# Strassen products in the second up product and in both down products, quad-shaped down weights, and the squares of x after the first product

## The chip, the cores and the metric

The kernel runs on one core of a Trainium2 chip. The core has a matrix engine (PE), a vector engine (DVE), a scalar engine (ACT), a general engine (POOL) and a queue engine (SP) that issues the transfers; each works through its own instructions in a fixed order and waits for the others by semaphores. The metric is the device time of one execution in microseconds; smaller is better. Before the change it is 2578.58 us, the median of three runs (2578.54 to 2579.13).

## What is computed

The reference is two transformer-like blocks in float32, one after the other, on 256 rows of 2048 columns. The change touches the feed-forward parts of both and the first norm. Cut to these:

```python
# first block
h = rmsnorm(x, norm_mix_g)
proj = h @ w_in
...                                  # two kinds of attention, cross attention
hf = rmsnorm(x, norm_ffn_g)
x = x + (silu(hf @ w_gate) * (hf @ w_up)) @ w_down       # 2048 -> 5632 -> 2048
x = rmsnorm(x, norm_f_g)
# second block
...                                  # gating unit, linear recurrence, w_out
h = rmsnorm(x, norm2_g)
up = causal_dwconv(h @ ffn_w_up, ffn_conv_w, ffn_conv_b)  # 2048 -> 2 x 6144
gate, val = split(up)
x = x + (gelu(gate) * val) @ ffn_w_down                   # 6144 -> 2048
x = rmsnorm(x, final_g)
```

## The kernel before

**Every product in three matmuls.** A float32 operand is split in a high part, rounded to the matrix engine's fast format, and a low part, the rest. `mm3` (L195 to L197) adds high times high, high times low and low times high. So each product of a 128 x 128 block of activations with a 128 x 512 block of weights is three matmuls of 128 x 512.

**Weights.** Each transfer (`fetch`, L279) brings a tile `w` of 128 x 2048, 1 MB. `push` cuts it in pieces of 128 x 1024 and splits each: ACT casts the high part `wh` (L177), DVE subtracts to get the low part `wl` (L178). `half` keeps the piece in use and four more ahead of it; `wh` and `wl` have five buffers each, so a cast waits until the matmuls of the piece five places back are done. The list `seq` sets the order of all tiles.

**A quad.** In the two up products (`w_gu`: gate and up of the first block, `w_uv`: of the second) one tile `w` holds two blocks of 128 rows by two blocks of 512 columns (one of the gate, one of the up half). With two blocks of tokens and two blocks of rows this is a 2 x 2 by 2 x 2 block product. Of kind "N" it takes 8 block products, 24 matmuls, and two weight pieces (0 and 1). Of kind "S" it takes 7, by Strassen's scheme, 21 matmuls, and four weight pieces: "a" (128 x 1024, raw), "c" (128 x 512, raw, its split in plain `r` tiles) and "b" and "d" (128 x 1024, sums in the tiles `wt`, made by DVE at L307, L311 and L312). An S quad also needs sums of activations, which the class `Quad` makes (L119 to L126). Strings of eight letters say which of a group's eight quads is which: `KINDS` "NSNSNSNN" for `w_gu`, 11 groups; `KINDS2` "NNNSNNNN" for `w_uv`, 12 groups.

**Up groups.** `quad_group` runs `gemm_q` over eight quads into four accumulators of the pool `psg` (tiles `pg`) and three of the pool `pss` (tiles `pp`); each pool has four banks. When the last S quad is through, `early` reads three of them (L460 to L462); at the group's end `finish` reads the others in five DVE operations (L468 to L474).

**Down products.** `w_down` and `w_down2` are taken in parts of the hidden width, `PARTS` and `PARTS2`, three each, the down product of a part after its up groups. Before the change they are plain: `gemm_tm` (four groups of 512 columns, two `pg` accumulators each, so that two groups fit in the four banks), and `add_x` (L511) adds the two results to x. No Strassen there. The activations for a part are transposed and split by `ffn_pairs` (first block) or, after the convolution, by `conv_pairs` (second block, lines L1122, L1125, L1137, L1143); these run as generators, one step at each `tick`, beside the next group's matmuls.

**The start.** `x_gen` loads x transposed in eight tiles of 128 x 512; `load_split` splits each for the first product (L180 on ACT, L181 on DVE), squares it on ACT (L552) and has POOL add the square to a sum (L554). The sum gives the first norm's factors.

**What sets the order.** The program is written for all engines at once; a scheduler that simulates time while building decides in which order each engine's instructions stand. On the chip that order is fixed.

## Time and profile before

| what | value |
|---|---|
| median of the runs | 2578.58 us |
| the profiled execution itself | 2578.38 us |
| its span, first to last instruction | 2576.7 us |
| PE, instructions | 12209 |
| DVE, instructions | 2257 |
| granted clock of PE over the span | 0.999 |
| time of the first up product (`w_gu`), one group | 42.4 us |
| time of the second up product (`w_uv`), one group | 44.8 us |
| bytes read from memory | 486.39 MB |

The profile is of one execution. A page gives busy times and shares; the windows view gives the same for chosen stretches, in us from the start of the span; the lines view groups instructions by source line and gives the mean duration of one, and after the second bar the time in which the engine was idle before them, with what it waited for; the timeline gives single instructions with their start and duration. An instruction's duration is not the time until the next one may start: both PE and DVE start the next one earlier, so rates are read from the distances of starts.

### The profile page before, as it was taken

How to read it: one execution, taken by the hardware profiler on the slowest of the kernel's cores; microseconds unless marked ns; L12 is line 12 of the kernel's file. 1: busy time of each engine (PE TensorE's matmuls, PEld its weight loads, DVE VectorE, ACT ScalarE, POOL GpSimd, SP SyncE). 2: the span in 40 equal slices, each digit the busy share in tenths (PEclk: the TensorE clock that was granted, in tenths of full speed). 3: DMA queues.
4: the chain of work that ended last, by engine and by line, in shares of the span. 5: the costliest groups of instructions: out<-in, count | busy, mean ns of one | idle time of the engine just before them, and what ended most of it. 6: DMA issues, size and time to landing. Idle time of an engine off the chain costs nothing.

```text
span 2576.7 us, 31159 instructions
## 1 busy us (share of the span) xinstructions
PE 2557.1 (99%) x12209; PEld 2144.2 (83%) x12209; DVE 1813.8 (70%) x2257; ACT 1397.2 (54%) x1863; POOL 39.5 (2%) x41
## 2 busy tenths in 40 slices
PE   8999999999999999999999999999999999999998
PEld 7888888888888888888888888888888888888887
DVE  7666566556569875887588667866887578757874
ACT  6555554455456553555455555665565456535654
POOL 2000010000000000000000000000000000000000
PEclk9999999999999999999999999999999999999999
DMA  6455555554454555555555564555555554555553
GB/s 258 164 180 204 203 206 182 194 180 164 147 180 180 213 197 195 196 201 197 192 194 213 196 221 163 186 190 184 192 187 190 190 191 178 195 193 194 182 212 131
DMA packets 72723, 490.51 MB, mean 190 GB/s; under 512 B 8192, under 2 KB 8320, under 8 KB 14592
## 3 DMA queue, kind: packets, MB, share of 16 engines
q1 hardware_dynamic: 72576, 488.52, 53.1%
q8 instruction: 96, 1.57, 0.2%
q14 instruction: 51, 0.42, 0.0%
HBM read 486.39 MB, written 2.10 MB: 190 GB/s over the span
## 4 chain that ended last, share of the span: by engine, by line
PE 98%; issue 0%; DVE 0%; ACT 0%; DMA 0%; POOL 0%; SPq 0%; ACTq 0%; POOLq 0%; DVEq 0%
PE pg L195 25%; PE pg L197 25%; PE pg L196 25%; PE pg L364 10%; PE pg L368 5%; PE pp L197 2%; PE pp L196 2%; PE pp L195 2%; PE pp L188 1%; PE pp L1137 1%; DMA w<-in_w_in_f_dram 0%; DVE r L181 0%; DVE wl L178 0%; PE pp L958 0%; PE pp L1010 0%
## 5 line engine op out<-in xcount | busy, mean ns | idle before, releaser
L178 DVE TENSOR_TENSOR wl<-w,wh 128x1024 fp32r<-128x1024 f32 x854 | 1044.5, 1225 | 601.2 <-ACT wh L177 596.1
L177 ACT CAST wh<-w 128x1024 fp32r<-128x1024 f32 x854 | 897.6, 1052 | 872.7 <-PE pg L197 696.0
L196 PE MATMUL pg<-wl,r 128*128 128x512 f32 x2783 | 1085.1, 390 | 0.0
L197 PE MATMUL pg<-wh,r 128*128 128x512 f32 x2783 | 1081.0, 390 | 0.0
L195 PE MATMUL pg<-wh,r 128*128 128x512 f32 x2783 | 1075.5, 391 | 0.0
L197 PEld LDWEIGHTS pg<-wh,r 128*128 128x128 f32 x2783 | 522.4, 188 | 108.2
L196 PEld LDWEIGHTS pg<-wl,r 128*128 128x128 f32 x2783 | 522.6, 188 | 107.3
L195 PEld LDWEIGHTS pg<-wh,r 128*128 128x128 f32 x2783 | 522.6, 188 | 106.6
L364 PE MATMUL pg<-r,wh 128*128 128x512 f32 x1152 | 311.9, 397 | 10.9 <-ACT wh L177 7.2
L364 PEld LDWEIGHTS pg<-r,wh 128*128 128x128 f32 x1152 | 201.7, 190 | 43.5 <-ACT wh L177 7.2
L368 PEld LDWEIGHTS pg<-r,wl 128*128 128x128 f32 x1152 | 168.7, 190 | 17.9
L368 PE MATMUL pg<-r,wl 128*128 128x256 f32 x1152 | 176.8, 284 | 0.0
L178 DVE TENSOR_TENSOR wl<-wt,wh 128x1024 fp32r<-128x1024 f32 x90 | 109.7, 1219 | 39.6 <-ACT wh L177 39.0
L177 ACT CAST wh<-wt 128x1024 fp32r<-128x1024 f32 x90 | 94.7, 1052 | 68.0 <-PE pg L197 40.5
L1125 DVE SCALAR_TENSOR_TENSOR f<-pp,pr,f 128x255 f32<-128x255 f32 x192 | 90.4, 478 | 13.7 <-ACT f L1122 11.7
L1122 ACT ACTIVATE f<-pp,pr 128x256 f32<-128x256 f32 x96 | 53.3, 561 | 33.0 <-PE pp L1137 16.9
L177 ACT CAST r<-f 128x512 fp32r<-128x512 f32 (+1 forms) x88 | 51.5, 585 | 14.9 <-DVE f L484 8.7
L178 DVE TENSOR_TENSOR r<-f,r 128x512 fp32r<-128x512 f32 (+1 forms) x88 | 56.6, 643 | 3.5 <-ACT r L177 2.8
L195 PE MATMUL pp<-wh,r 128*128 128x512 f32 x147 | 58.3, 400 | 0.0
L197 PE MATMUL pp<-wh,r 128*128 128x512 f32 x147 | 57.3, 390 | 0.0
L196 PE MATMUL pp<-wl,r 128*128 128x512 f32 x147 | 57.3, 390 | 0.0
L307 DVE TENSOR_TENSOR wt<-w 128x1024 f32<-128x1024 f32 x45 | 54.8, 1218 | 2.6 <-DMA w<-in_w_gu_dram 2.6
(193 smaller groups left out, 1465.1 us busy)
## 6 DMA issues: line engine op xcount, KB each, us to landing
w<-in_w_uv_dram SPq DMA_DIRECT2D x96, 1024.0 KB, 4.8
w<-in_w_down_dram SPq DMA_DIRECT2D x92, 1024.0 KB, 4.8
w<-in_w_gu_dram SPq DMA_DIRECT2D x88, 1024.0 KB, 4.8
w<-in_w_in_t_dram SPq DMA_DIRECT2D x40, 1024.0 KB, 4.8
w<-in_w_in_f_dram SPq DMA_DIRECT2D x39, 1024.0 KB, 4.8
w<-in_w_o_dram SPq DMA_DIRECT2D x16, 1024.0 KB, 4.8
w<-in_w_xk_dram SPq DMA_DIRECT2D x16, 1024.0 KB, 4.8
w<-in_w_xv_dram SPq DMA_DIRECT2D x16, 1024.0 KB, 4.8
```

Of the source, the lines that this page charges most:

```text
L177: A.copy(hi, src)
L178: V.tensor_tensor(lo, src, hi.bitcast(F32), ALU.subtract)
L188: T.transpose(pt[:, k, t * P:(t + 1) * P], src[t][:, c + k * P:c + (k + 1) * P], ident)
L195: T.matmul(out, lhsT=lh[0], rhs=rh[0], start=start, stop=False)
L196: T.matmul(out, lhsT=lh[0], rhs=rh[1], start=False, stop=False)
L197: T.matmul(out, lhsT=lh[1], rhs=rh[0], start=False, stop=stop)
L307: V.tensor_tensor(sums["b"], b[:, 3:4, :].to_broadcast([P, 2, 512]), b[:, 0:3:2, :], ALU.subtract)
L364: T.matmul(ps[m], lhsT=hi[k][:, m * P:(m + 1) * P], rhs=ops[k].both(k % 2), start=begin and k == 0, stop=stop, skip_group_check=True)
L368: T.matmul(ps[m][:, S:], lhsT=lo[k][:, m * P:(m + 1) * P], rhs=ops[k].hi(k % 2), start=False, stop=False, skip_group_check=True)
L1122: A.activation(y[:, j, :], z[:, j, :], AF.Identity, scale=col("ffn_conv_w_2", 192 + c), bias=col("ffn_conv_b_2", c))
L1125: V.scalar_tensor_tensor(y[:, j, d:], z[:, j, :S - d], col("ffn_conv_w_2", 96 * (2 - d) + c), y[:, j, d:], ALU.mult, ALU.add)
L1137: T.transpose(pt[:, k, t * P:(t + 1) * P], z[t][:, (2 * p + k) * P:(2 * p + k + 1) * P], ident)
```

## The change

- `KINDS2` has two S quads per group of `w_uv` instead of one (places 2 and 5 instead of 3).
- Both down weights are stored as quads too, of two blocks of 128 rows by two blocks of 512 neighbouring columns. `gemm_sum` takes two groups of 1024 columns instead of four of 512. In the first two parts, places 3 and 5 of each eight quads are S (`KINDS_DOWN`); in the last part all are N. The last 1024 columns of the last part of `w_down2` stay plain, as `w_down2_t`.
- `add_quads` takes the place of `add_x`: it uses four `pg` accumulators and, with S quads, four `pp` ones. When the last S quad is through, `early` copies one, makes four combinations and adds them to x; at the end four more additions go to x. From the first to the last S quad of a down group no generator steps.
- Activations that meet an S quad of a down product are made as a `Quad` (the old kind "N" of that class is now called "D").
- The convolution's generator steps faster for the last up group of a part (`pause` 1 instead of 2).
- The squares of x come after the first product's matmuls in the program, and DVE adds them instead of POOL.

```diff
-KINDS2 = "NNNSNNNN"
+KINDS2 = "NNSNNSNN"
+KINDS_DOWN = "NNNSNSNN"
...
-        seq += [(w_down, g, u) for g in range(4) for u in range(g0, g1)]
+        seq += [(w_down, g, u) for g in range(2) for u in range(2 * g0, 2 * g1)]
...
-        seq += [(w_down2, g, u) for g in range(4) for u in range(g0, g1)]
+        seq += [(w_down2, g, u) for g in range(2) for u in range(2 * g0, 2 * g1)] if g0 < PARTS2[-1][0] else []
+    g0, g1 = PARTS2[-1]
+    seq += [(w_down2, 0, u) for u in range(2 * g0, 2 * g1)]
+    seq += [(w_down2_t, g, u) for g in range(2) for u in range(g1 - g0)]
...
     def kind(w, u):
+        if w is w_down or w is w_down2:
+            return KINDS_DOWN[u % 8] if u < 2 * (PARTS if w is w_down else PARTS2)[-1][0] else "N"
...
+    def gemm_sum(wap, g, acts, k0, sums_done):
+        M = {}
+        n = len(acts)
+        ks = [kind(wap, k0 + u) for u in range(n)]
+        first, end = ks.index("S") if "S" in ks else n, n - ks[::-1].index("S") if "S" in ks else 0
...
+        def prod(m, a, b):
+            if m not in M:
+                M[m] = gps() if m > 10 else sps()
+            done[m] += 1
+            mm3(M[m], a, b, done[m] == 1, done[m] == total[m])
+
+        for u in range(n):
+            if u == first:
+                for v in range(first, end):
+                    need(acts, v)
+            a = need(acts, u)
+            if ks[u] == "N":
+                plan = [(0, [(11, a.blk(0, 0), 0), (11, a.blk(1, 0), 1), (21, a.blk(0, 1), 0), (21, a.blk(1, 1), 1)]),
+                        (1, [(22, a.blk(1, 1), 0), (22, a.blk(0, 1), 1), (12, a.blk(1, 0), 0), (12, a.blk(0, 0), 1)])]
+            else:
+                plan = [("a", [(1, a.blk(0, 0), 0), (11, a.blk(1, 0), 1)]),
+                        ("c", [(12, a.sums(3), 0)]),
+                        ("b", [(5, a.sums(0), 0), (7, a.sums(2), 1)]),
+                        ("d", [(6, a.sums(1), 0), (21, a.blk(1, 1), 1)])]
+            for i, ops in plan:
+                hi, lo = half(wap, g, k0 + u, i, 512)
+                for m, x, b in ops:
+                    prod(m, x, (hi[b], lo[b]))
+                if not first <= u < end:
+                    tick()
+            if u == end - 1:
+                sums_done(M)
+        return M
...
+    def add_quads(wap, g, acts, k0):
+        def early(M):
+            m, u2, u3, v = (flat(ft()) for _ in range(4))
+            A.copy(m, M[1])
+            V.tensor_tensor(u2, M[6], m, ALU.add)
+            V.tensor_tensor(u3, M[7], u2, ALU.add)
+            V.tensor_tensor(u2, M[5], u2, ALU.add)
+            V.tensor_tensor(v, M[5], u3, ALU.add)
+            for x, f in zip(parts, (m, u3, v, u2)):
+                V.tensor_tensor(x, x, f, ALU.add)
+
+        parts = [xs(0, 2 * g), xs(1, 2 * g), xs(1, 2 * g + 1), xs(0, 2 * g + 1)]
+        M = gemm_sum(wap, g, acts, k0, early)
+        for x, i in zip(parts, (11, 21, 22, 12)):
+            V.tensor_tensor(x, x, M[i], ALU.add)
...
     def load_split(f, gname, p, sq):
         a = Pair(True).fill(f, [col(gname, 2 * p + j) for j in range(2)])
+        if sq is not None:
+            square(f, sq)
+        return a
+
+    def square(f, sq):
         s = ft()
         A.activation(s, f, AF.Square)
-        if sq:
-            G.tensor_tensor(sq[0], sq[0], s, ALU.add)
-        else:
-            sq.append(s)
-        return a
+        sq.append(s)
+
+    def sum_squares(sq, eng):
+        while len(sq) > 1:
+            eng.tensor_tensor(sq[0], sq[0], sq.pop(1), ALU.add)
...
     ps_q = gemm_fm(w_in_f, 0, h_a)
     al = big(alibi)
+    for f in fs:
+        square(f, sq1)
+        sum_squares(sq1, V)
...
-        for g in range(4):
-            add_x(gemm_tm(w_down, g, acts, g0), g)
-            if g1 == PARTS[-1][1]:
-                spawn(next_in(g, h2_a, sq_f, gg, second_norm), 1)
+        for g in range(2):
+            add_quads(w_down, g, acts, 2 * g0)
+            if last_part:
+                for i in range(2):
+                    spawn(next_in(2 * g + i, h2_a, sq_f, gg, second_norm), 1 + 2 * i)
...
+            if sums and KINDS_DOWN[i + p] == "S":
+                acts[i + p] = Quad("S", y[0], psum=False)
+            else:
+                acts[i + p] = Pair(False).fill(y[0])
...
-            for g in range(4):
-                add_x(gemm_tm(w_down2, g, acts, g0), g)
+            for g in range(2):
+                add_quads(w_down2, g, acts, 2 * g0)
...
+    add_quads(w_down2, 0, acts, 2 * PARTS2[-1][0])
     for g in range(3):
-        add_x(gemm_tm(w_down2, g, acts, PARTS2[-1][0]), g)
+        if g == 2:
+            add_x(gemm_tm(w_down2_t, 0, acts), 2)
```

How the scheduler places this, at three places. In the rows, names with a number are buffers: `wl` and `wh` the low and high parts of a weight piece, `wt` the summed weights, `r` split activations (or the small piece "c"), `f` plain tiles, `pp` and `pg` accumulators, `xt` the rows of x.

DVE at the start, before, from the third weight tile's second piece on (`w_144` to `w_324` are weight tiles of the first product, `f_177` to `f_219` tiles of x, L181 their split):

```order
L178 TENSOR_TENSOR wl_191<-w_144,wh_190 128x1024
L181 SCALAR_TENSOR_TENSOR r_221<-f_177,pr,r_221 128x256
L181 SCALAR_TENSOR_TENSOR r_222<-f_177,pr,r_222 128x256
L181 SCALAR_TENSOR_TENSOR r_250<-f_179,pr,r_250 128x256
L181 SCALAR_TENSOR_TENSOR r_251<-f_179,pr,r_251 128x256
L178 TENSOR_TENSOR wl_231<-w_175,wh_230 128x1024
L178 TENSOR_TENSOR wl_269<-w_175,wh_268 128x1024
L181 SCALAR_TENSOR_TENSOR r_259<-f_219,pr,r_259 128x256
L181 SCALAR_TENSOR_TENSOR r_260<-f_219,pr,r_260 128x256
L178 TENSOR_TENSOR wl_327<-w_324,wh_326 128x1024
```

DVE at the same place in the changed kernel (the same lines are L182 and L185 there; L628 are the sums of squares, which stood on POOL at L554):

```order
L182 TENSOR_TENSOR wl_246<-w_167,wh_245 128x1024
L185 SCALAR_TENSOR_TENSOR r_239<-f_205,pr,r_239 128x256
L185 SCALAR_TENSOR_TENSOR r_240<-f_205,pr,r_240 128x256
L628 TENSOR_TENSOR f_269<-f_269,f_271 128x512
L628 TENSOR_TENSOR f_269<-f_269,f_274 128x512
L628 TENSOR_TENSOR f_269<-f_269,f_277 128x512
L628 TENSOR_TENSOR f_269<-f_269,f_280 128x512
L628 TENSOR_TENSOR f_269<-f_269,f_283 128x512
L182 TENSOR_TENSOR wl_327<-w_324,wh_326 128x1024
L628 TENSOR_TENSOR f_269<-f_269,f_286 128x512
L182 TENSOR_TENSOR wl_350<-w_324,wh_349 128x1024
```

The additions now stand on DVE, behind the last split of x and before the weights of the second product's group; nothing of them stands among the splits of x any more, on no engine.

DVE in the first down product of the second block, before, where the first two groups' results are added to x (L511) among weight pieces (`w_16228` to `w_16368`):

```order
L178 TENSOR_TENSOR wl_16265<-w_16262,wh_16264 128x1024
L511 TENSOR_TENSOR xt<-xt,pg_16026 128x512
L511 TENSOR_TENSOR xt<-xt,pg_16027 128x512
L178 TENSOR_TENSOR wl_16281<-w_16262,wh_16280 128x1024
L178 TENSOR_TENSOR wl_16299<-w_16296,wh_16298 128x1024
L178 TENSOR_TENSOR wl_16315<-w_16296,wh_16314 128x1024
```

DVE there in the changed kernel, from the sums of the first down group on (L567 to L570 the combinations, L572 and L577 the additions to x):

```order
L567 TENSOR_TENSOR f_16573<-pp_16492,f_16572 128x512
L572 TENSOR_TENSOR xt<-xt,f_16572 128x512
L568 TENSOR_TENSOR f_16574<-pp_16481,f_16573 128x512
L182 TENSOR_TENSOR wl_16588<-w_16585,wh_16587 128x1024
L569 TENSOR_TENSOR f_16573<-pp_16477,f_16573 128x512
L570 TENSOR_TENSOR f_16575<-pp_16477,f_16574 128x512
L572 TENSOR_TENSOR xt<-xt,f_16574 128x512
L577 TENSOR_TENSOR xt<-xt,pg_16286 128x512
L182 TENSOR_TENSOR wl_16604<-w_16585,wh_16603 128x1024
L572 TENSOR_TENSOR xt<-xt,f_16573 128x512
L572 TENSOR_TENSOR xt<-xt,f_16575 128x512
```

Where two additions stood between weight pieces, eight operations of the same size stand among two pieces, and they read accumulators of both pools.

More of the change, by code (lines that the diff above doesn't have):

```diff
@@ L50, in tile_kernel @@
                 lru_wa, lru_wx, w_in_f, w_in_t, w_o, w_xq, w_xk, w_xv, w_xo, w_gu, w_down,
-                w_in2_f, w_in2_t, w_out2, w_uv, w_down2, out):
+                w_in2_f, w_in2_t, w_out2, w_uv, w_down2, w_down2_t, out):
     nc = tc.nc
@@ L94, in both, with blk @@
             return flat(self.t[k])
+        def blk(self, k, t):
+            return self.hi(k)[:, t * P:(t + 1) * P], self.lo(k)[:, t * P:(t + 1) * P]
         def fill(self, src, gcols=None):
@@ L105, in tile_kernel, with __init__ @@
     class Quad:
-        def __init__(self, kind, src, gcols=None):
-            f = ft()
-            for k in range(2):
-                if gcols is not None:
+        def __init__(self, kind, src, gcols=None, psum=True):
+            f = ft() if psum else src
+            if gcols is not None:
+                for k in range(2):
                     A.activation(f[:, k, :], src[:, k, :], AF.Identity, scale=gcols[k])
-            if gcols is None:
+            elif psum:
                 A.copy(f, src)
@@ L119, in __init__ @@
             e = ft()
-            if kind == "N":
+            if kind == "D":
                 x = rt()
@@ L451, in gemm_q @@
         return M
+    def gemm_sum(wap, g, acts, k0, sums_done):
[3 more added lines that the diff above has]
+        first, end = ks.index("S") if "S" in ks else n, n - ks[::-1].index("S") if "S" in ks else 0
+        ns, nn = ks.count("S"), ks.count("N")
+        total = {11: 2 * nn + ns, 12: 2 * nn + ns, 21: 2 * nn + ns, 22: 2 * nn, 1: ns, 5: ns, 6: ns, 7: ns}
+        done = dict.fromkeys(total, 0)
+        def prod(m, a, b):
[25 more added lines that the diff above has]
+        return M
     def quad_group(wap, g, acts):
@@ L517, in operands @@
             acts[2 * g + p] = xpose_split(xrow, P * c, [gcols[:, c + j:c + j + 1] for j in range(2)], True,
-                                          None if kinds is None else kinds[2 * g + p])
+                                          None if kinds is None else kinds[2 * g + p].replace("N", "D"))
             yield
@@ L757, in mem_gen @@
             hm_a[p] = load_split(fm[p], "norm_mem_g", p, sqm)
+            sum_squares(sqm, G)
             if p + 2 < KT // 2:
@@ L851, in tile_kernel, with ffn_pairs @@
     h2_a = [None] * 8
-    def ffn_pairs(s, acts, i):
+    def ffn_pairs(s, acts, i, sums):
         for p in range(2):
-            acts[i + p] = xpose_split(s, 256 * p)
+            strassen = sums and KINDS_DOWN[i + p] == "S"
+            acts[i + p] = xpose_split(s, 256 * p, quad="S" if strassen else None)
             yield
@@ L866, in tile_kernel @@
     for g0, g1 in PARTS:
+        last_part = g1 == PARTS[-1][1]
         acts = [None] * (2 * (g1 - g0))
@@ L874, in tile_kernel @@
                 V.scalar_tensor_tensor(s[t], up, r[t], s[t], ALU.mult, ALU.mult)
-            spawn(ffn_pairs(s, acts, 2 * (g - g0)))
-        for g in range(4):
-            add_x(gemm_tm(w_down, g, acts, g0), g)
-            if g1 == PARTS[-1][1]:
-                spawn(next_in(g, h2_a, sq_f, gg, second_norm), 1)
+            spawn(ffn_pairs(s, acts, 2 * (g - g0), not last_part))
+        for g in range(2):
[3 more added lines that the diff above has]
+                    spawn(next_in(2 * g + i, h2_a, sq_f, gg, second_norm), 1 + 2 * i)
     def tok(ins):
@@ L1127, in conv3, with conv_pairs @@
         return y
-    def conv_pairs(gate, val, g, acts, i):
+    def conv_pairs(gate, val, g, acts, i, pause, sums):
         for p in range(2):
@@ L1139, in conv_pairs @@
                 y.append(conv3(pt, c0))
-                yield
-                yield
+                for _ in range(pause):
+                    yield
             A.activation(y[0], y[0], AF.Gelu_apprx_tanh)
             V.tensor_tensor(y[0], y[0], y[1], ALU.mult)
-            acts[i + p] = Pair(False).fill(y[0])
-            yield
+            if sums and KINDS_DOWN[i + p] == "S":
+                acts[i + p] = Quad("S", y[0], psum=False)
+            else:
+                acts[i + p] = Pair(False).fill(y[0])
     sq_o = Sq(4)
@@ L1160, in tile_kernel @@
                 scaled(t, val)
-            spawn(conv_pairs(gate, val, g, acts, 2 * (g - g0)))
+            spawn(conv_pairs(gate, val, g, acts, 2 * (g - g0), 1 if g == g1 - 1 else 2, g1 < PARTS2[-1][1]))
         if g1 < PARTS2[-1][1]:
-            for g in range(4):
-                add_x(gemm_tm(w_down2, g, acts, g0), g)
+            for g in range(2):
+                add_quads(w_down2, g, acts, 2 * g0)
     gf = []
@@ L1178, in tile_kernel @@
     ps = [sps(), sps()]
-    second = gemm_tm(w_down2, 3, acts, PARTS2[-1][0], ps, TAIL)
+    second = gemm_tm(w_down2_t, 1, acts, 0, ps, TAIL)
     for t in range(2):
@@ L1235, in wquad, with pairs @@
         return np.ascontiguousarray(q).reshape(q.shape[0], q.shape[1], P, 2048)
+    def pairs(w):
+        w = w.reshape(w.shape[0], -1, 2, 512)
+        return [w[:, :, i].reshape(w.shape[0], -1) for i in range(2)]
     par = np.concatenate(
```

7 lines of the change are left out of this document (4 added, 3 removed).

## The prediction

> **What bounds the kernel now.** I read the page first: the busy times and the chain that ended last.
>
> ```profile
> PE 2557.1 (99%) x12209; PEld 2144.2 (83%) x12209; DVE 1813.8 (70%) x2257; ACT 1397.2 (54%) x1863; POOL 39.5 (2%) x41
> PE 98%; issue 0%; DVE 0%; ACT 0%; DMA 0%; POOL 0%; SPq 0%; ACTq 0%; POOLq 0%; DVEq 0%
> ```
>
> The chain of waits is matmuls for 98% of the span, so a matmul less is time less, as long as DVE keeps up. PE's 99% alone would not say that: matmuls overlap, and the pace comes from windows. Those of the stages that the change touches (length; then busy time and count for PE, PEld, DVE, ACT, POOL; clock; DMA):
>
> ```profile
> 970.46:1013.98 43.52, 43.52 (x193) 36.04 (x192) 21.99 (x21) 16.88 (x16) 0.00 (x0) 1.00 0.54 194
> 863.02:905.42 42.40, 42.40 (x192) 35.18 (x191) 37.55 (x43) 23.97 (x27) 0.00 (x0) 1.00 0.55 199
> 947.79:992.22 44.43, 44.43 (x201) 36.87 (x200) 25.02 (x26) 17.84 (x18) 0.00 (x0) 1.00 0.53 190
> 1902.17:1946.93 44.76, 44.76 (x206) 37.04 (x205) 36.77 (x49) 27.33 (x35) 0.00 (x0) 1.00 0.54 189
> 1946.93:1992.31 45.38, 45.38 (x210) 37.64 (x208) 31.69 (x42) 24.18 (x30) 0.00 (x0) 1.00 0.53 185
> 1992.31:2035.83 43.52, 43.52 (x194) 36.04 (x192) 22.00 (x21) 17.50 (x17) 0.00 (x0) 1.00 0.55 194
> ```
>
> The first is two groups of a down product, 8 units of 24 matmuls each, nothing else: 43.52 us for 192 matmuls (the count has one more, which began earlier), **0.2267 us per matmul of 128 x 512**. The second is a gate-and-up group of the first block with three S quads: 5 x 24 + 3 x 21 = 183 matmuls give 41.49 us, its 8 transposes the other 0.9; so PE lost nothing there, though DVE was busy for 37.55 of 42.40 us (89%). The fourth is a group of the second up product (DVE 82%), the fifth and sixth are halves of a down product after it.
>
> **The change part by part.** *Matmuls.* Each S quad saves one product, three matmuls. Second up product: one more S quad in 12 groups, 36 matmuls. Down products: two S quads in 2 groups of 2 parts, in 2 blocks, 16 quads, 48 matmuls. The instructions of the changed program agree: 84 fewer matmuls of 128 x 512, transposes as before. 84 x 0.2267 = **19.0 us**.
>
> *What DVE pays.* Steps from start to start in a stretch where DVE did not wait:
>
> ```profile
> 863.73 0.68 DVE L473 TENSOR_TENSOR f<-pg,f 128x512 f32<-128x512 f32 x1
> 864.33 1.21 DVE L307 TENSOR_TENSOR wt<-w 128x1024 f32<-128x1024 f32 x1
> 865.46 1.22 DVE L178 TENSOR_TENSOR wl<-wt,wh 128x1024 fp32r<-128x1024 f32 x1
> 866.60 0.68 DVE L474 TENSOR_TENSOR f<-pg,f 128x512 f32<-128x512 f32 x1
> 867.20 0.74 DVE L874 SCALAR_TENSOR_TENSOR f<-f,s,f 128x512 f32<-128x512 f32 x1
> 867.86 0.68 DVE L311 TENSOR_TENSOR wt<-wt,w 128x512 f32<-128x512 f32 x1
> 868.46 1.22 DVE L178 TENSOR_TENSOR wl<-w,wh 128x1024 fp32r<-128x1024 f32 x1
> ```
>
> So an operation on 128 x 1024 takes DVE 1.14 us and one on 128 x 512 0.60. An N quad costs two splits, 2.28. An S quad costs three splits, one small split, the 128 x 1024 sum and two 128 x 512 sums: 3.42 + 0.60 + 1.13 + 1.20 = 6.35. One more S quad is +4.07 us on DVE and -0.68 on PE. A down group with S quads has also eight more additions, four combinations and four to x, 8 x 0.60 = 4.8. Activations for an S quad of a down product cost one more split, 0.60, and four sums of 128 x 128, each below the sum of 128 x 256 in this row (0.42):
>
> ```profile
> L122 DVE TENSOR_TENSOR f<-f 128x256 f32<-128x256 f32 x12 | 5.0, 418 | 0.0
> ```
>
> so at most 2.3 per such pair. ACT gains 1.5 casts per S quad and stays below two thirds.
>
> *Does it fit?* Stage by stage, DVE of before plus the addition, against PE of before less the matmuls:
> - First block, up group whose step makes a pair of sums: 37.55 + 2.3 = 39.9 of 42.4. Its first down group: 25.02 + 8.14 + 4.8 = 38.0 of 43.1. Both fit.
> - Second block, up group: 36.77 + 4.07 = 40.8 of 44.1, and with a pair of sums 43.1, 98%.
> - Second block, first down group of parts 1 and 2: 31.69 + 8.14 + 4.8 = 44.6 of 44.0, 101%; the group behind it 22.00 + 12.9 = 34.9 of 42.2.
>
> So only at two places (last up group and first down group of the first two parts) is DVE full: 87.7 of 88.1 us. The lead hides it if it is whole: four pieces of 12 matmuls, 10.9 us of PE work, against an overload of 0.6. What it does not hide is an accumulator that is read late because its addition stands behind weight pieces in DVE's fixed order; queued behind it are the next splits, and PE waits for both. No row shows DVE that full. Between 0 and, if half of an up group's present idle time remained, some 4.6 us at each place (worked out below), I take 0.5 each, **+1.0 us** together, nearer to nothing because the 89% window lost nothing.
>
> *The start.* What PE waited for in the first 30 us, the window up to its last wait, and DVE and POOL there:
>
> ```profile
> PE pg L364 <- DVE r L181: 3.1, 4, 1.1
> 7.23:20.07 12.84, 9.73 (x35) 6.85 (x36) 12.74 (x15) 12.28 (x22) 6.60 (x5) 1.00 1.04 414
> 7.21 2.54 DVE L178 TENSOR_TENSOR wl<-w,wh 128x1024 fp32r<-128x1024 f32 x2 [0.97 <-ACT wh L177]
> 9.67 3.72 DVE L181 SCALAR_TENSOR_TENSOR r<-f,pr,r 128x256 fp32r<-128x256 f32 x4
> 15.58 1.50 DVE L181 SCALAR_TENSOR_TENSOR r<-f,pr,r 128x256 fp32r<-128x256 f32 x1
> 18.25 1.26 DVE L181 SCALAR_TENSOR_TENSOR r<-f,pr,r 128x256 fp32r<-128x256 f32 x3
> 9.90 2.81 POOL L554 TENSOR_TENSOR f<-f,f 128x512 f32<-128x512 f32 x2 [9.40 <-ACT f L552]
> 14.75 3.47 POOL L554 TENSOR_TENSOR f<-f,f 128x512 f32<-128x512 f32 x2 [2.04 <-ACT f L552]
> ```
>
> Four splits of x took 3.72 us and one took 1.50 while POOL added squares; three took 1.26 between POOL's additions. PE's four waits, 3.1 us, end on these splits. The change takes away POOL's additions and ACT's eight squares from this stretch. The first wait (up to 1.1) stays, since it stands behind the two weight splits at 7.21, before POOL begins; I take **-2.0 us** of the 3.1. Ends: 0, because the transfers are 104% busy there and may be the next to be late, and -5, because the 35 matmuls of this window also ran below pace: at most 35 x 0.2267 = 7.9 us of the 12.84. The seven additions, now 7 x 0.60 = 4.2 us on DVE, and the squares in one run on ACT, come after the last split of x. Their cover is this window, where DVE rests for 3.3 of 10 us and PE lost nothing:
>
> ```profile
> 30.00:40.00 10.00, 10.00 (x61) 8.85 (x60) 6.71 (x12) 4.23 (x8) 0.71 (x1) 1.00 0.69 252
> ```
>
> If that cover were gone, it would cost up to the 0.9 that exceeds it. The first factors of the norm come later, but the accumulators are emptied before the factors are used, so PE does not wait for them.
>
> A rule bears on the start: the Trainium skill, page "SBUF — State Buffer", section "Who interferes with whom", says that a DVE instruction with two inputs in SBUF and a POOL instruction that reads SBUF block each other for the whole instruction. The slow splits agree with it. By it alone DVE would get back all of POOL's 6.6 us in that window and the 3.1 us would go entirely, which makes the sum 1.1 us lower than mine.
>
> *The rest* is worth nothing: the bytes are the same (SP issues as many transfers), the last 512 columns end the program as before, and the operands of the next stage after the first block's last down group are taken in the order in which they are made.
>
> **Sum.** From the profiled execution's own 2578.38 us: -19.0 - 2.0 + 1.0 = 2558.4. The median of the runs is 0.2 above that execution, so **2558.5 us**.
>
> **Rivals.**
>
> *Evacuation comes to light; slower.* A down product now fills all four banks of both pools, and the next one needs the same banks. If the additions at its end stop PE, each of the 11 quad products (6 in the first block, 5 in the second) costs four of 0.60, 2.4 us, and each of the 8 with S quads another 4.8: 26 + 38 = 64 us, and 2578.4 - 21.0 + 64 = **2621 us**. It decides from 21.0 / 11 = 1.9 us per product. Against it: the up groups fill four `pg` banks too, their five readings are on DVE, and the gate window above lost nothing; two of the four accumulators end a half quad, 12 x 0.2267 = 2.7 us, before the others. For it: DVE is fuller now. The Trainium skill, page "Perfetto Trace Analysis", section "Matmuls", advises that matmul groups rotate through different banks so that one group's evacuation lies beside the next one's matmuls; the plain down groups of before did that, the quads do not, and the up groups show no loss from it. Chance 0.04.
>
> *DVE becomes the bound at its two full places.* DVE's order is fixed, and it idles where its next split's cast is not there:
>
> ```profile
> L178 DVE TENSOR_TENSOR wl<-w,wh 128x1024 fp32r<-128x1024 f32 x13 | 15.8, 1220 | 3.7 <-ACT wh L177 3.7
> L178 DVE TENSOR_TENSOR wl<-wt,wh 128x1024 fp32r<-128x1024 f32 x7 | 8.5, 1217 | 1.2 <-ACT wh L177 1.2
> ```
>
> That is the gate group at 863.02, 4.9 us of idle time. If half of it stays in each of the two groups of a full place, DVE needs 87.7 + 4.9 = 92.6 of 88.1 us: +4.5 at each of two places, 9.0 for the 1.0 above, **2566.5 us**. For it: in-order waits can't all vanish. Against it: these casts wait for PE to free a buffer, so they are the sign of a full lead, and DVE's busy and idle time always add up to PE's window. Chance 0.16.
>
> *The pace is not the matmul's.* If the weight load set it, a matmul less would be worth only the duration of its load, in this row:
>
> ```profile
> L196 PEld LDWEIGHTS pg<-wl,r 128*128 128x128 f32 x2783 | 522.6, 188 | 107.3
> ```
>
> 84 x 0.188 = 15.8 us, and with the other terms 2578.4 - 15.8 - 1.0 = **2561.6 us**. Against it: the loads idle for 107.3 us ahead of this group alone, and the down window's starts lie 0.227 apart where a load lasts 0.188. Chance 0.04.
>
> *The change doesn't do what it says.* The count of the built program speaks against it: 84 matmuls fewer, 28 sums of 128 x 1024 more. The start alone may not: with a gain of 0 there the sum is 2560.4, with 5 us it is 2555.4. Both belong to the forecast.
>
> **How the numbers follow.** The forecast, matmuls saved at full pace and a start of 0 to 5 us, with up to 3 us given back, has 0.76: from 2554.5 to 2562. DVE at its full places has 0.16, around 2566.5; if all of its idle time stayed there instead of half, 2 x 9.4 less the 1.0 already in would make it 2576.2, no change. The pace has 0.04, evacuation 0.04. The range runs from 2554.5 to 2567.5: below it lies 0.04 of the forecast, above it half of the DVE case and the evacuation, 0.12. A change of 0.2% (5.2 us) is about what a measurement of this kernel can tell from none. Faster: 0.76 and 0.04 from forecast and pace, 0.13 from DVE, 0.93. Same: 0.03, the DVE case with all idle time left. Slower: 0.04, the evacuation.
>
> **What would show it.** PE's count falls by 84 to 12125 and the distance of matmuls in a down group stays at 0.227. An up group of the second block takes 44.1 us instead of 44.8, the halves of a down product behind it 44.0 and 42.2 instead of 45.4 and 43.5, and those of the first block 43.1 and 42.2. The last up group and the first down group of the second block's first two parts are where PE may wait, for `wl` or for a `pg` bank; idle time of `wl` for its cast should shrink there. At the start, the splits of x take 0.4 us each and PE's waits for them fall to about one. DVE's busy time grows by 28 x 4.07 + 8 x 4.8 + 4.2 us and the sums of activations, to about 1985 us. I am wrong if an up group of the first block gets longer than 42.4 us (then evacuation or the buffers are at work, not DVE's load), if the full places lose more than 3 us each, or if the start's wait moves to a transfer.

## The result, and the profile after

The changed kernel takes **2594.78 us** (median of four runs, 2591.9 to 2595.21) against 2578.56 (2578.51 to 2579.13) on the same chip: ratio 1.006, 95% interval 1.0043 to 1.0077. It is slower by 0.6%, where 2558.5 us was forecast. Its profiled execution took 2595.21 us, with a span of 2593.4.

The page of the changed kernel, the same two lines as were shown of before (busy time, share of the span and instructions of each engine; shares of the chain that ended last):

```profile
PE 2550.0 (98%) x12125; PEld 2135.0 (82%) x12125; DVE 1966.8 (76%) x2511; ACT 1448.1 (56%) x1939; POOL 27.5 (1%) x34
PE 95%; DVE 2%; DMA 1%; ACT 1%; issue 1%; SPq 0%; POOL 0%; ACTq 0%; POOLq 0%; DVEq 0%
```

The matmuls that were to go are gone: 12125 instead of 12209. But the chain, 98% PE before, is now 95% PE and 2% DVE. The waits view of PE says where (what waited, for what; us in total, times, longest):

```profile
PE pg L199 <- DVE f L517: 23.1, 5, 7.9
...
PE pp L235 <- DVE f L233: 3.0, 1, 3.0
```

Both lines are new. The line numbers of the changed kernel lie above those of before: its L517 is the first reading of a `pg` accumulator at the end of an up group (L468 before), L509 to L511 the copy and the two additions that precede it (L460 to L462), L316, L320 and L321 the weight sums of an S quad (L307, L311, L312), L182 the low parts (L178), L1215 the convolution's transposes (L1137).

All five waits for L517 lie at the end of an up group of the second block. Here is the first, in the timeline of PE and then of ACT and DVE (start, duration, instruction):

```profile
1899.19 0.39 PE L201 MATMUL pg<-wh,r 128*128 128x512 f32 x1
1907.45 0.76 PE L199 MATMUL pg<-wh,r 128*128 128x512 f32 x1 [7.87 <-DVE f L517]
1908.01 0.63 PE L200 MATMUL pg<-wl,r 128*128 128x512 f32 x1
1908.44 0.63 PE L201 MATMUL pg<-wh,r 128*128 128x512 f32 x1
```

```profile
1904.04 0.62 ACT L181 CAST r<-f 128x512 fp32r<-128x512 f32 x1 [3.33 <-DVE f L135]
1904.56 0.58 ACT L509 COPY f<-pp 128x512 f32<-128x512 f32 x1
```

```profile
1897.30 0.69 DVE L1221 TENSOR_TENSOR f<-f,f 128x512 f32<-128x512 f32 x1
1897.90 1.22 DVE L316 TENSOR_TENSOR wt<-w 128x1024 f32<-128x1024 f32 x1
...
1900.04 0.68 DVE L320 TENSOR_TENSOR wt<-wt,w 128x512 f32<-128x512 f32 x1
...
1903.12 0.68 DVE L321 TENSOR_TENSOR wt<-wt,w 128x512 f32<-128x512 f32 x1
1903.72 0.28 DVE L135 TENSOR_TENSOR f<-f,f 128x128 f32<-128x128 f32 x1
...
1905.30 0.68 DVE L510 TENSOR_TENSOR f<-pp,f 128x512 f32<-128x512 f32 x1
1906.01 0.69 DVE L511 TENSOR_TENSOR f<-pp,f 128x512 f32<-128x512 f32 x1
1906.62 0.68 DVE L517 TENSOR_TENSOR f<-pg,f 128x512 f32<-128x512 f32 x1
```

The group's last matmul starts at 1899.19. The next group needs the bank that L517 empties, and L517 comes at 1906.62. Ahead of it stand the end of the convolution (L1221), all the sums of the *next* group's first S quad (L316, L320, L321), and the sums for the activations of the down product (up to L135). ACT has copied nothing yet either: its copy L509 stands behind the cast of those activations.

The windows view shows that busy time does not tell this. A window of the changed kernel (length; busy time and count of PE, PEld, DVE, ACT, POOL; clock; DMA), then the same window of the kernel `after_p1` below, which has no such wait:

```profile
1860.00:1905.00 45.00, 39.58 (x181) 32.39 (x179) 38.48 (x53) 26.27 (x35) 0.00 (x0) 0.96 0.52 189
```

```profile
1860.00:1905.00 45.00, 44.95 (x206) 36.88 (x205) 40.26 (x58) 28.74 (x37) 0.00 (x0) 1.00 0.52 188
```

DVE is busy for 38.48 of 45 us where PE loses most, and for 40.26 where it loses nothing (and more of the program fits in the same 45 us).

The long waits cost more than themselves. Behind the one above, matmuls start 0.43 us apart instead of 0.227. In the changed kernel the next wait ends at the first row here; in the kernel `after_guard` below, the same group lies between the second and the third:

```profile
1955.04 0.47 PE L199 MATMUL pg<-wh,r 128*128 128x512 f32 x1 [1.09 <-DVE f L517]
```

```profile
1898.55 0.47 PE L199 MATMUL pg<-wh,r 128*128 128x512 f32 x1 [1.09 <-DVE f L518]
1943.98 0.47 PE L199 MATMUL pg<-wh,r 128*128 128x512 f32 x1 [1.09 <-DVE f L518]
```

1955.04 - 1907.45 - 1.09 = 46.5 us against 1943.98 - 1898.55 - 1.09 = 44.3: 2.2 us on top of the wait of 7.9. Behind the second long wait (7.7 us) the same reckoning, between the waits that end at 2179.66 and 2227.62 and, in `after_guard`, at 2161.88 and 2207.34, gives 2.5. Behind the third (5.4 us) no later wait marks the end of the group; taken as the mean of the other two it is another 2.3, an estimate. Together 7.0.

The start, in the timeline of PE:

```profile
34.41 0.95 PE L635 MATMUL pp<-ones,f 128*128 128x1 f32 x8
38.33 1.22 PE L235 MATMUL pp<-f,ones 128*128 128x256 f32 x2 [2.97 <-DVE f L233]
```

L635 sums the squares over the partitions. Its result goes through DVE, POOL and DVE again before PE can spread the factors over the partitions (L235), and in PE's fixed order nothing stands between the two. PE's 301st matmul, which lies well behind this place, starts at 71.78 us, where it started at 67.85 before: the start costs 3.9 us net.

So the profiled executions, 2578.38 and 2595.21, differ by +16.8, and the parts are: -19.0 for the matmuls, +23.1 for the five waits, +7.0 for the slow matmuls behind three of them, +3.9 at the start: +15.0. The 1.8 us that are left were not followed.

### The profile page after: what moved, and what is told of

It is laid out like the page before. It is cut to its first block, busy times and chain, and to the rows that moved or that the text cites. A ratio compares the mean times of both kernels' runs of the same rounds, so it can differ in the third digit from the quotient of the medians.

```text
span 2593.4 us, 31365 instructions
## 1 busy us (share of the span) xinstructions
PE 2550.0 (98%) x12125; PEld 2135.0 (82%) x12125; DVE 1966.8 (76%) x2511; ACT 1448.1 (56%) x1939; POOL 27.5 (1%) x34
## 4 chain that ended last, share of the span: by engine, by line
PE 95%; DVE 2%; DMA 1%; ACT 1%; issue 1%; SPq 0%; POOL 0%; ACTq 0%; POOLq 0%; DVEq 0%
PE pg L199 23%; PE pg L200 23%; PE pg L201 23%; PE pg L373 10%; PE pg L377 5%; PE pp L201 3%; PE pp L200 3%; PE pp L199 3%; PE pp L192 1%; DVE wl L182 1%; PE pp L1215 1%; ACT wh L181 0%; DMA w<-in_w_gu_dram 0%; DMA w<-in_w_in_f_dram 0%; DMA w<-in_w_uv_dram 0%
## 5 line engine op out<-in xcount | busy, mean ns | idle before, releaser
L182 DVE TENSOR_TENSOR wl<-w,wh 128x1024 fp32r<-128x1024 f32 x826 | 1006.4, 1223 | 437.9 <-ACT wh L181 431.8
L181 ACT CAST wh<-w 128x1024 fp32r<-128x1024 f32 x826 | 864.7, 1052 | 729.3 <-PE pg L201 519.8
L199 PE MATMUL pg<-wh,r 128*128 128x512 f32 x2627 | 1008.3, 393 | 23.5 <-DVE f L517 23.1
L200 PE MATMUL pg<-wl,r 128*128 128x512 f32 x2627 | 1027.4, 391 | 0.0
L201 PE MATMUL pg<-wh,r 128*128 128x512 f32 x2627 | 1023.6, 391 | 0.0
L199 PEld LDWEIGHTS pg<-wh,r 128*128 128x128 f32 x2627 | 495.0, 188 | 127.5 <-issue 25.1
L201 PEld LDWEIGHTS pg<-wh,r 128*128 128x128 f32 x2627 | 494.7, 188 | 103.2
L181 ACT CAST wh<-wt 128x1024 fp32r<-128x1024 f32 x146 | 153.7, 1053 | 138.6 <-PE pg L201 93.0
L182 DVE TENSOR_TENSOR wl<-wt,wh 128x1024 fp32r<-128x1024 f32 x146 | 178.1, 1222 | 53.6 <-ACT wh L181 51.6
L316 DVE TENSOR_TENSOR wt<-w 128x1024 f32<-128x1024 f32 x73 | 89.1, 1221 | 16.9 <-DMA w<-in_w_uv_dram 8.2
L1203 DVE SCALAR_TENSOR_TENSOR f<-pp,pr,f 128x255 f32<-128x255 f32 x192 | 90.8, 478 | 12.8 <-ACT f L1200 11.0
L201 PE MATMUL pp<-wh,r 128*128 128x512 f32 x247 | 96.7, 392 | 0.0
L200 PE MATMUL pp<-wl,r 128*128 128x512 f32 x247 | 96.2, 389 | 0.0
L199 PE MATMUL pp<-wh,r 128*128 128x512 f32 x247 | 96.0, 392 | 0.0
L181 ACT CAST r<-f 128x512 fp32r<-128x512 f32 (+1 forms) x100 | 59.2, 592 | 32.3 <-DVE f L1221 10.4
L181 ACT CAST r<-w 128x512 fp32r<-128x512 f32 x83 | 50.6, 616 | 38.2 <-DMA w<-in_w_gu_dram 22.0
```

The source lines that it names most:

```text
L181: A.copy(hi, src)
L182: V.tensor_tensor(lo, src, hi.bitcast(F32), ALU.subtract)
L199: T.matmul(out, lhsT=lh[0], rhs=rh[0], start=start, stop=False)
L200: T.matmul(out, lhsT=lh[0], rhs=rh[1], start=False, stop=False)
L201: T.matmul(out, lhsT=lh[1], rhs=rh[0], start=False, stop=stop)
L316: V.tensor_tensor(sums["b"], b[:, 3:4, :].to_broadcast([P, 2, 512]), b[:, 0:3:2, :], ALU.subtract)
```

## The experiments

Each ratio is to the kernel before on the same chip. Three chips were used, and the median of the kernel before was 2578.74 to 2578.86 us on them. The theories in the expectations are as they stood before each run.

**One part of the change alone.** `up_only` is the kernel before with the second S quad in the second up product; `down_only` is the changed kernel without it and with the squares as before; `squares_only` is the kernel before with the later squares.

```diff
 up_only, to the kernel before:
-KINDS2 = "NNNSNNNN"
+KINDS2 = "NNSNNSNN"
 down_only, to the changed kernel (and the squares undone):
-KINDS2 = "NNSNNSNN"
+KINDS2 = "NNNSNNNN"
```

> The kernel before with KINDS2 = NNSNNSNN alone: 36 matmuls less, 8.2 us. Theory A (DVE falls behind in the second block's up groups, and the evacuation of the group's accumulators stands late in its order): PE waits of 1 to 8 us before a group's first accumulator, near the third boundary of each part, as in the changed kernel; 2578.6 - 8.2 + 20 to 30 = 2590 to 2600 us. Theory B (the down quads, their sums of activations and their eight additions make the backlog): no such waits, 2570.4 us.

> The changed kernel with the old KINDS2 (one S quad per up group) and the squares of x as before: 48 matmuls less, 10.9 us. Theory A: no wait of PE for a first accumulator over 1 us, 2567.7 us. Theory B: the waits of 1 to 8 us are there, 2567.7 + 20 to 30 us.

> The kernel before with the squares of x later and added by DVE, nothing else. Theory A (the factors come later and PE stands in its order before the small matmul that spreads them): PE's waits for the splits of x fall to about 1.2 us, and a new wait of 3 us with slow matmuls behind it appears at 35 us; 2578.6 + 3 to 5 = 2582 to 2584 us. The prediction's step: 2576.6 us.

`up_only`: 2627.9 us, ratio 1.0192 (1.0175 to 1.0209). `down_only`: 2568.75, ratio 0.996 (0.9945 to 0.9975). `squares_only`: 2580.53, ratio 1.0006 (0.9997 to 1.0016). PE's waits for such readings in the first two, and the new wait of the third:

```profile
PE pg L195 <- DVE f L468: 35.4, 9, 4.4
```

```profile
...
PE pg L199 <- DVE f L522: 0.4, 1, 0.4
```

```profile
PE pp L231 <- DVE f L229: 3.0, 1, 3.0
```

The down products do what they were to do: 48 matmuls x 0.2267 = 10.9 us, 10.1 measured, and no wait at the end of an up group of the second block. The loss is the second S quad's, and alone it is larger than in the whole change: nine waits, three in each part, at the end of every group beside which a convolution runs (a part's first group has none). That is 28 us above the range of theory A, whose waits it shows. One thing beside the letters differs from the changed kernel: there `conv_pairs` also leaves out the `yield` after each pair of tiles, which `up_only` still has. Whether that is why `up_only` loses at all three ends was not tried. The later squares bring the wait of 3.0 us at the start; alone their price, 1.7 us, lies too close to no change to be told, and below what was expected.

**Other places for the S quads.** `up_places` is the changed kernel with the last S quad two places earlier; `up_36` and `up_34` are `up_only` with other places.

```diff
 up_places, to the changed kernel:
-KINDS2 = "NNSNNSNN"
+KINDS2 = "NSNSNNNN"
 up_36, and up_34, to up_only:
-KINDS2 = "NNSNNSNN"
+KINDS2 = "NNNSNNSN"
+KINDS2 = "NNNSSNNN"
```

> The changed kernel with KINDS2 = NSNSNNNN: as many S quads, the second one earlier in the group. If the amount of work on DVE makes the waits, they stay: 2590 to 2597 us. If the late place of the second S quad makes them (its sums are read just before the group's end), they go: 24 us and the slow matmuls behind them, 2565 to 2572 us.

> The kernel before with KINDS2 = NNNSNNSN: as many S quads as the up-only kernel, both one place later, so that the next group's first weight sum stands behind the first reading of the accumulators in the order; the S sums' four banks are held as long (places 3 to 6 instead of 2 to 5) and are read even later. Theory H: few or no waits, 2570 to 2576 us. Theory L, or one that blames the banks held or the late second S quad: as the up-only kernel, above 2600 us.

> The kernel before with KINDS2 = NNNSSNNN: the S sums' banks are held for two quads only, but two of the three weight sums still stand ahead of the reading. Theory H: waits, smaller than in the up-only kernel (1.7 of 2.3 us of hoisted sums), 2580 to 2610 us. A theory that blames the banks held by the S sums: no waits, 2570 us.

`up_places`: 2597.75 us, ratio 1.0072 (1.0057 to 1.0088). `up_36`: 2615.74, 1.0145 (1.0129 to 1.016). `up_34`: 2627.61, 1.0187 (1.0172 to 1.0203). `up_places` still waits and comes out 0.8 us above the range for that; `up_36` lies where the rivals of theory H put it, and `up_34` fits neither of its theories. It is not how late the last S quad stands (place 3 loses like place 5), and not for how long the sums hold their banks (two neighbouring places lose like two that are three apart).

**The weight sums kept behind the reading.** An edge for the scheduler: the sum "b" of the next group's S quad may not stand ahead of the last reading of this group's accumulators. `up_guard` is `up_only` with it, `after_guard` the changed kernel with it.

```diff
+                with tc.issue_after(read[0].ins) if read[0] else ExitStack():
-                V.tensor_tensor(sums["b"], ...)
+                    V.tensor_tensor(sums["b"], ...)
...
-            V.tensor_tensor(u2, M[3], u2, ALU.add)
+            read[0] = V.tensor_tensor(u2, M[3], u2, ALU.add)
```

> The up-only kernel with one more order edge: the weight sum of an S quad may not stand on DVE ahead of the last reading of the group before. Theory H (the next group's three weight sums, hoisted ahead of the reading of the accumulators, make PE wait): the waits for a group's first accumulator go, 2570 to 2573 us. Theory L (too much work on DVE in a group with two S quads and the convolution): waits stay, above 2600 us.

> The changed kernel with the same edge. Theory H: the waits of 8.0, 7.9 and 5.6 us go (those of 1.3, where no sum stood ahead, may stay), with the slow matmuls behind them: 2562 to 2566 us. Theory L: 2590 to 2600 us.

`up_guard`: 2602.23 us, ratio 1.0092 (1.0075 to 1.0109). `after_guard`: **2568.15**, ratio 0.9958 (0.9943 to 0.9973). Waits for the first reading, of `up_guard` and of `after_guard`:

```profile
PE pg L195 <- DVE f L469: 20.1, 9, 3.7
```

```profile
PE pg L199 <- DVE f L518: 4.3, 4, 1.1
```

In the changed kernel the long waits are gone with the hoisted sums: one edge gives 26.6 us back, 2 less than the least that was expected. But in `up_guard` more than half of the waiting is left with no sum ahead of the reading. What stands there is the convolution's last step and its split, and on ACT the copy of the first sum is behind both. So the next question was why the convolution ends so late.

**The convolution one step faster.** Between the halves of a convolution the generator pauses; the changed kernel has 2 steps there, 1 in the last group of a part. `up_guard_p1` is `up_guard`, and `after_p1` the changed kernel *without any edge*, each with 1 everywhere. `guard_sq` is `after_guard` with the squares as before, and `guard_sq_p1` is `guard_sq` with 1 everywhere.

```diff
 after_p1, to the changed kernel:
-            spawn(conv_pairs(gate, val, g, acts, 2 * (g - g0), 1 if g == g1 - 1 else 2, g1 < PARTS2[-1][1]))
+            spawn(conv_pairs(gate, val, g, acts, 2 * (g - g0), 1, g1 < PARTS2[-1][1]))
 guard_sq, to after_guard:
-                h_a[n] = load_split(fs[n], "norm_mix_g", n, None)
+                h_a[n] = load_split(fs[n], "norm_mix_g", n, sq1)
+                sum_squares(sq1, G)
...
-    for f in fs:
-        square(f, sq1)
-        sum_squares(sq1, V)
```

> The second up product's two Strassen pairs alone with the edge on the weight sum (2602.23; nine waits of PE at the group ends, 1.2 or 3.9 us each), and one step less between the convolution's halves. Theory C (the convolution's last step and split ahead of the reading): the nine waits fall below 0.6 us, and the time to 2570 to 2580. Theory W (weight pieces ahead of the reading): waits of 1 us and more stay at most of the nine ends, and the time between 2592 and 2608.

> The changed kernel without any edge, with one step less between the convolution's halves in every group. If the hoisted weight sums are what makes PE wait 8 us at the end of the second group of a part, they stay ahead of the reading there, and the time stays between 2585 and 2600. If it was the convolution that pushed the reading back, the waits fall below 1.5 us each and the time below 2575.

> The changed kernel with the two parts undone or mended that the earlier runs put a price on: the edge that keeps the next group's weight sum behind the last reading of the accumulators, and the squares of x at the start as they were before the change. After the edge alone the time was 2568.15, and the start of that kernel still had the 3.1 us wait of PE for the first factors, with slow matmuls behind it. Theory A (that wait costs some 4 us net): 2563.5 to 2565.5. Rival (the later squares cost as little as they did alone, where the ratio was 1.0006): 2566 to 2568.5.

> The kernel guard_sq with one step less between the convolution's halves in every group (pause 1 everywhere, where all but a part's last group had 2), so that the convolution's last step and its split stand earlier in DVE's order. Theory C (what is left of the waits at the group ends, four of 1.25 us, comes of the convolution's last step and split standing ahead of the first reading): no wait above 0.6 us is left there, 2 to 6 us below guard_sq, about 2560 to 2562. Theory W (it comes of the weight pieces that stand ahead of the reading, wherever the convolution is): the waits stay between 1 and 4 us and the time within 2 us of guard_sq or above it.

`up_guard_p1`: 2570.49 us, ratio 0.9967 (0.9954 to 0.998). `after_p1`: **2565.12**, 0.9947 (0.9932 to 0.9962). `guard_sq`: 2565.84, 0.9949 (0.9934 to 0.9964), between the ranges of its two theories. `guard_sq_p1`: **2561.39**, 0.9931 (0.9915 to 0.9948), the fastest of all. In none of the three with pause 1 does PE wait for the first reading at all. My expectation for `after_p1` was wrong: I took the hoisted sums for a cause of their own, and they are not. With the convolution out of the way the reading moves ahead of them by itself, as DVE's timeline of `after_p1` at the same group end shows:

```profile
1894.82 0.68 DVE L510 TENSOR_TENSOR f<-pp,f 128x512 f32<-128x512 f32 x1
...
1897.16 0.68 DVE L517 TENSOR_TENSOR f<-pg,f 128x512 f32<-128x512 f32 x1
...
1900.08 1.21 DVE L316 TENSOR_TENSOR wt<-w 128x1024 f32<-128x1024 f32 x1
```

**Why the convolution ended late.** Four transposed tiles per group feed the convolution, and they take banks of `pss`, the pool of four from which an up group takes three for its sums. The trace does not show banks, but PE's order shows when each `pp` tile is first written. This is one group of the changed kernel, and the same group with the S quads in places 4 and 5 (position on PE; L1215 are the transposes, L199 the first matmul into a sum):

```
8776 L1215 MATMUL pp_15535<-ident,f_15499 128x128
8821 L1215 MATMUL pp_15584<-ident,f_15135 128x128
8829 L199 MATMUL pp_15618<-wh_15515,r_14454 128x512
8835 L1215 MATMUL pp_15638<-ident,f_15499 128x128
8846 L199 MATMUL pp_15659<-wh_15568,r_14463 128x512
8888 L199 MATMUL pp_15667<-wh_15596,r_14463 128x512
8926 L1215 MATMUL pp_15694<-ident,f_15135 128x128
```

```
8787 L1215 MATMUL pp_15533<-ident,f_15499 128x128
8809 L1215 MATMUL pp_15581<-ident,f_15135 128x128
8837 L1215 MATMUL pp_15635<-ident,f_15499 128x128
8865 L1215 MATMUL pp_15682<-ident,f_15135 128x128
8881 L199 MATMUL pp_15718<-wh_15611,r_14632 128x512
8893 L199 MATMUL pp_15757<-wh_15666,r_14641 128x512
8915 L199 MATMUL pp_15765<-wh_15694,r_14641 128x512
```

In the first, three sums and the third transposed tile hold the four banks, so the fourth can only follow when the convolution has read the third. The program as built names the banks: there the sums lie in 6, 5 and 4, and the third and the fourth tile both in 7. In the second all four transposes come first, in 5, 7, 4 and 6, with the pause as it was. `up_45` and `after_45` are `up_only` and the changed kernel with these places. `p1_sq` is `after_p1` with the squares as before.

```diff
 after_45, to the changed kernel (up_45 the same, to up_only):
-KINDS2 = "NNSNNSNN"
+KINDS2 = "NNNNSSNN"
```

> The second up product's two Strassen pairs alone, in places 4 and 5 of a group instead of 2 and 5, with the convolution's pauses as before (2). By the order of TensorE's instructions the convolution's four transposed tiles then all take a bank before the sums' three (M1, M7, M6) do, which in places 2 and 5, 3 and 4, 3 and 6, and 1 and 3 they did not. Theory B (the last transposes must wait while the sums hold three of the four banks, and so the convolution ends late and the reading of the accumulators with it): no wait of PE above 1.5 us at the nine group ends, 2570 to 2580. Rival (with pause 2 the convolution is too slow beside two Strassen pairs, wherever these stand): waits of 2 to 5 us stay, 2605 to 2630.

> The changed kernel with its up product's Strassen pairs in places 4 and 5 and nothing else changed: no edge, pause as in the change. Theory B: the waits of 8 us for the first reading are gone or below 1.5 us, 2564 to 2574. Rival (the pause, or the work of two Strassen pairs on DVE, makes the loss): 2585 to 2600.

> The changed kernel with pause 1 in every group and the squares at the start as before the change, without the edge on the weight sums. If the edge does nothing once the convolution ends early, and the start is worth 2 to 4 us as between the kernels with the edge: 2560.5 to 2563. If the edge still holds something back: 2563.5 or more.

`up_45`: 2571.17 us, ratio 0.9971 (0.9959 to 0.9982): 56.7 us below `up_only` by two letters, and no wait for a reading in its list. `after_45`: 2574.73, 0.9985 (0.9976 to 0.9995), 0.7 above the range. `p1_sq`: 2563.18, 0.9943 (0.9928 to 0.9958), 0.2 above its first range. What the edge is still worth lies within the 1.8 us to `guard_sq_p1`, which ran on another chip. The transposes of the group that ends at 1899 (1897 in the second kernel), in PE's timelines of the changed kernel and of `after_45`:

```profile
1858.61 0.49 PE L1215 MATMUL pp<-ident,f 128*128 128x128 f32 x3
1866.69 0.60 PE L1215 MATMUL pp<-ident,f 128*128 128x128 f32 x4
1869.44 0.60 PE L1215 MATMUL pp<-ident,f 128*128 128x128 f32 x4
1889.64 0.60 PE L1215 MATMUL pp<-ident,f 128*128 128x128 f32 x4
```

```profile
1857.29 0.60 PE L1215 MATMUL pp<-ident,f 128*128 128x128 f32 x4
1861.86 0.60 PE L1215 MATMUL pp<-ident,f 128*128 128x128 f32 x4
1867.77 0.60 PE L1215 MATMUL pp<-ident,f 128*128 128x128 f32 x4
1873.70 0.60 PE L1215 MATMUL pp<-ident,f 128*128 128x128 f32 x4
```

The last tile is transposed 20 us behind the third in the one, 6 us in the other. In the first, DVE reads the third tile until 1885.1 (L1203), and the fourth follows 4.5 us later. A shared bank alone is no loss yet: in the group before, the third and the fourth tile also lie in one bank, but the fourth is transposed at 1842.33, 14 us before that group's end, and PE does not wait there. At 1889.64 it is 9.6 us before the last matmul. What `after_45` still loses is two waits of 3.7 us at the end of a part's last up group (its waits view, then DVE's timeline):

```profile
PE pg L199 <- DVE f L517: 7.5, 2, 3.7
```

```profile
1942.75 1.23 DVE L182 TENSOR_TENSOR wl<-w,wh 128x1024 fp32r<-128x1024 f32 x1 [0.50 <-ACT wh L181]
1943.89 0.68 DVE L511 TENSOR_TENSOR f<-pp,f 128x512 f32<-128x512 f32 x1
1944.49 0.68 DVE L517 TENSOR_TENSOR f<-pg,f 128x512 f32<-128x512 f32 x1
```

There a low part that itself waits for a cast stands between the readings. Why it stands there was not tried.

So the chain is: sums and transposes share four banks; beside the second S quad the last transposes come late; the convolution's end and its split come late; the copies and additions that empty the accumulators stand behind it; and, once they are late, ready work for the next group (the hoisted sums) goes ahead of them too. The runs show each end of it: earlier transposes alone take the loss away, all of it by the pause, and by the places all of it in `up_45` and all but two waits in `after_45`; keeping the hoisted sums back takes most of it away in the changed kernel. That the fourth tile needs the third one's bank stands in the program; how much of the 20 us is the wait for that bank was not measured.

## Why the prediction was wrong, point by point

*The matmuls: right.* 84 fewer, as counted. Where nothing waits, they bring what was worked out: the up product's 36 x 0.2267 = 8.2 us came out as 8.4 in `up_guard_p1` and 7.6 in `up_45`; the down products' 10.9 as 10.1 in `down_only`.

*"Does it fit?": the step that failed.* I compared sums of DVE's busy time with PE's time, stage by stage, and let the second up group pass because 40.8 of 44.1 us "fits"; only the two places with 87.7 of 88.1 us were charged, 0.5 us each. The text named the right mechanism ("an accumulator that is read late because its addition stands behind weight pieces in DVE's fixed order") and put it at too few places and at the wrong price. It happened at five ends of up groups, for 23.1 us and 7.0 of slow matmuls, not 1.0. The two waits of 1.09 us stand where the text had put them, between the last up group and the down product; the three long ones stand between one up group and the next, where it had charged nothing. Busy time could not have shown it; the order of the changed program could: L316, L320 and L321 stand ahead of L517 there.

*The cover for the price, a gate group that lost nothing at 89%, was another kind of group.* It has three S quads, but beside it only two transposed tiles and no convolution. And in the second block before the change the transposes were late already; that cost nothing, because the copy of the first sum still came 13 us before the next group begins at 1902.17 (PE's and ACT's timelines of before):

```profile
1887.88 0.60 PE L1137 MATMUL pp<-ident,f 128*128 128x128 f32 x4
```

```profile
1888.98 0.57 ACT L460 COPY f<-pp 128x512 f32<-128x512 f32 x1
```

*The rival "evacuation comes to light": the right sign, the wrong product.* It was put at the down quads, which lost nothing in the changed kernel (in `after_p1` one of them has a wait of 1.05 us for an addition to x, L577), and dismissed because the up groups showed no loss. The up groups were where it came, and its bound of 1.9 us per product was passed at three ends (7.9, 7.7, 5.4).

*The rival "DVE becomes the bound": not it.* With DVE as busy or busier, `after_p1` loses nothing at the ends of the up groups. DVE's total is 1966.8 us, 18 below the 1985 worked out.

*The start: half right.* The splits are undisturbed as forecast, and PE does more in the window up to the last of their waits, 44 matmuls where it was 35, 9 x 0.2267 = 2.0 us (an answer for the line of the splits, with minimum, median and maximum in ns, and the window):

```profile
L185 DVE SCALAR_TENSOR_TENSOR r<-f,pr,r x16: 477/480/485, 5.4 to 24.5; 128x256 fp32r<-128x256 f32 x16
```

```profile
7.23:20.07 12.84, 11.52 (x44) 8.80 (x45) 10.24 (x16) 9.75 (x18) 0.00 (x0) 1.00 1.03 411
```

Wrong was "PE does not wait for them" of the factors. The accumulators are indeed emptied without the factors, but a matmul that spreads the factors stands in PE's own order, and it waited 3.0 us. Undoing the later squares gave 2.3 us (`after_guard` to `guard_sq`) and 1.9 (`after_p1` to `p1_sq`, whose runs overlap). So the term was about +2, not -2.0. In the profiled execution of the changed kernel it was +3.9: behind that wait the granted clock was 0.51 over 6.67 us, against 0.74 over 6.59 us in `after_p1`.

*The sum with both terms mended.* `guard_sq_p1` has the matmuls gone, no late reading and the old start. By the prediction's own terms that is 2578.6 - 19.0 = 2559.6; measured 2561.39. The 1.8 us between them were not followed.

## What to carry to other kernels

Whether an engine with a fixed order keeps up is not read from its busy time: look in the built order for what stands between a group's last matmul and the first reading of its accumulators, and count how far that reading is from the group's end before and after. Where accumulators share a pool of banks with something else, look at which of them come first, since a small tile that comes late (here four transposes of 128 x 128) can hold back all that follows it. And a matmul that needs a result of three engines in turn can cost PE their whole chain when no other matmuls stand between.

## What the runs showed of the hardware

After a long wait PE's granted clock is halved for several us (the clock column is the mean over the window). Windows of the changed kernel behind the wait of 7.87 us, and behind one of 1.09:

```profile
1907.45:1912.00 4.55, 4.55 (x11) 3.58 (x12) 2.24 (x4) 2.56 (x4) 0.00 (x0) 0.50 0.00 0
1912.00:1917.00 5.00, 5.00 (x26) 4.10 (x25) 1.19 (x2) 2.02 (x3) 0.00 (x0) 1.00 0.00 0
1955.00:1960.00 5.00, 4.96 (x22) 4.09 (x23) 5.00 (x7) 1.57 (x4) 0.00 (x0) 1.00 0.45 187
```

Behind its other two long waits (7.7 and 5.4 us) the clock reads 0.50 for 5.44 us from 2179.66 and for 4.67 us from 2450.08. And in `up_places`, three waits in PE's timeline, and the windows behind them:

```profile
1856.82 0.47 PE L199 MATMUL pg<-wh,r 128*128 128x512 f32 x1 [2.24 <-DVE f L517]
...
1954.80 0.73 PE L199 MATMUL pg<-wh,r 128*128 128x512 f32 x1 [2.76 <-DVE f L517]
...
2131.39 0.47 PE L199 MATMUL pg<-wh,r 128*128 128x512 f32 x1 [2.23 <-DVE f L517]
```

```profile
1857.00:1862.00 5.00, 5.00 (x25) 4.09 (x25) 4.97 (x7) 3.00 (x5) 0.00 (x0) 1.00 0.53 210
...
1954.90:1960.00 5.10, 5.10 (x16) 4.07 (x17) 3.88 (x6) 2.46 (x4) 0.00 (x0) 0.67 0.19 77
...
2131.50:2136.50 5.00, 5.00 (x15) 3.92 (x16) 4.41 (x6) 1.83 (x3) 0.00 (x0) 0.66 0.62 213
```

The clock column reads 0.50 where the wait was 7.87 us, 0.67 and 0.66 where it was 2.76 and 2.23, and 1.00 where it was 2.24 or 1.09. The Trainium skill, page "TensorE: Matmul & The Clock Gate", section "HAM oscillation — how this bites in real kernels", tells of the same drop to half speed and gives a gap of about 3.4 us as the limit; here waits of 2.76 and 2.23 us were enough. The length of the wait alone does not decide it, since 2.24 and 2.23 us went different ways in one trace; what does was not followed. Where the cost could be taken, behind the first two long waits of the changed kernel, it was 2.2 and 2.5 us on top of the wait.
